# Layer 1 of a two-layer encoder: ten column pairs in two passes of block products instead of nine in three with an ordinary column, and the residual read in twelve portions

## The chip, the cores and the metric

The kernel runs on one core of a Trainium2 chip. The metric is device time in microseconds (us) of one execution, as the median of several runs of one compiled program. The engines: PE is TensorE (matmuls), DVE is VectorE, ACT is ScalarE, POOL is GpSimd, SP is SyncE, which here only issues DMAs. Each engine takes its instructions in the order of its own queue.

## The reference, cut to what matters

Two layers over 384 tokens (256 of a prompt, 128 of running streams) and a model width of 2048. Layer 0 is attention and is not touched. Layer 1, whose projections and gate the change is about, is

```
def c_project(h, w_in1, ln_g, ln_b):
    p = jnp.einsum('bsd,dn->bsn', h, w_in1)
    u = p[..., :C_WIDTH]
    v = layernorm(p[..., C_WIDTH:2 * C_WIDTH], ln_g, ln_b)
    z = p[..., 2 * C_WIDTH:]
    return u, v, z
...
u, v, z = c_project(rmsnorm(hp, norm1_g), w_in1, sgu_ln_g, sgu_ln_b)
mixed = spatial_mix(v...)
hp = hp + jnp.einsum('bsn,nd->bsd', u * mixed * jax.nn.silu(z), w_out1)
```

with C_WIDTH = 4096, all in fp32; `w_in1` is 2048 x 12288.

## The kernel before

**Precision.** A matmul takes operands of a shorter format (fp32r). Each fp32 operand is split into a high part (a copy by ScalarE, L90 or L84) and a low part (source minus high, by VectorE, L91 or L86), and each product is three matmuls: high by high, high by low, low by high. A token block is 128 of the 384 tokens (tb 0, 1, 2). A column is 512 of the 12288 columns of `w_in1`, so u, v and z have eight each, numbered 0 to 7.

**An ordinary column** (`dense_nat`, or `eight`, which cuts it into steps) takes 16 rows of blocks of 128 along the contraction, each with 3 token blocks and 3 matmuls: 144 matmuls of 128x128 by 128x512. Its weights come as `raw` tiles of 128x512.

**A pair of columns** is computed by `seven`, for columns a0 and a1 at once, by a Strassen scheme of the Winograd kind: token blocks 0 and 1 and the two halves of the contraction make 2 x 2 blocks, and seven block products (1 to 7) do for eight. Token block 2 is done beside them with four block products, p and q for column a0 and two into one bank, s, for a1. A block product is taken over four depths u, with 6 matmuls each (`stream`): 11 products x 4 x 6 = 264 matmuls for a pair, where two ordinary columns take 288. The weights come in wide tiles `sraw` of 128x1024 (512 KB, `load2`), some are added to each other by VectorE (L970), and each is split (`split2`) into `shi` and `slo`, four buffers of each. The sums of token blocks that the scheme needs are made once, before the stage, by `token_sums`, from the transposed and normalised activations `h1c`, and stay in `slot` and `suml` tiles; `row` and `tsum` give a product its tokens. For v pairs the statistics of the layer norm follow each result (L1041), for pairs of z and u the SiLU of z (ScalarE, L1055) and the product with u (VectorE, L898); results go to DRAM through POOL's queue (`vd`, `gd`).

**The stage.** Columns 0 and 1 of v are ordinary (from about 700 us to 780 us in the profile), and `token_sums` runs between the steps of the second. Then comes the pair stage, 780 to 1396 us: three v pairs (columns 2 to 7), then NP = 6 pairs of z and u (columns 0 to 5). A pair takes three passes: `singles` (products 1, p, 2, q), `chain` (5, s, 6, 4) and `pair` (3, s, 7), each over the four depths and each followed by a closing that brings its banks to the results. Column 6 of z and u is ordinary, and its 32 steps of 9 matmuls are strewn between the steps of the pairs by `some` and the numbers in `mix`; their `raw` tiles come through POOL's queue.

**What sets the order.** `run` prepares a step (loads, additions, splits) and issues the matmuls of the step before it. Below that a scheduler of the framework places the instructions in each engine's queue by its own estimate of when their operands are ready; `tc.issue_after` forbids it to place an instruction ahead of another one. Loads of `sraw` go through SP's queue and wait there for the release of one of the buffers (8 of 4 KB a partition).

**After the stage** come column 7 of z and u (ordinary), the spatial mixing in `prepare` (whose steps are hooked to the steps of other work by `hooked`), and the last projection `out1` in four pieces. The residual, saved in DRAM (`h1d`) in four column blocks, is read back by `residual_back`: one block at hook 15 of column 7, three more at hooks 3, 7 and 10 of the first `out1`, three DMAs each (L1285).

## Time and profile before

| | |
|---|---|
| median of 3 runs | 1756.37 us (1752.81 to 1758.05) |
| the profiled execution | 1750.52 us |
| its span, first to last instruction | 1748.8 us |
| granted TensorE clock, mean | 0.998 |
| busy: PE, DVE, ACT, POOL | 1733.6, 1258.0, 803.5, 383.7 us |
| weight loads of PE (PEld, beside the matmuls) | 1433.6 us |
| DMA | 416.02 MB, mean 238 GB/s |

Durations and places are read in the profiled execution, whose own time lies 5.9 us below the median; differences are made against it. The page gives the share of the span in which each engine is busy; windows of the trace give the same for a stretch. A group of instructions is given by line, engine, operation, output and inputs, with count, busy time, mean duration, and the idle time before it with what ended it. In the timeline a row has start, duration, engine, line, and instruction. PE's ends are modelled and its matmuls overlap, so its rate is read from the starts.

### The profile page before, as it was taken

What the parts mean: (1) busy time and instruction counts of PE and PEld (TensorE: products, weight loads), DVE (VectorE), ACT (ScalarE), POOL (GpSimd) and SP (SyncE); (2) the same over time, 40 slices, a digit from 0 to 9 for tenths busy, and PEclk for the clock granted to TensorE, in tenths of its full rate; (3) what the DMA queues carried; (4) which work ended last, traced back from release to release, by engine and by line L of the source; (5) the groups of instructions that cost most, each with busy time, mean ns of one, the idle gap of its engine ahead of it and who ended that gap; (6) DMA issues with size and microseconds to landing.
All of it is one profiled execution on the core that took longest, in us unless ns stands there. A gap on an engine that the chain in (4) does not pass through costs nothing. (4 is left out here: it accounts for less than half of the span.)

```text
span 1748.8 us, 24034 instructions
## 1 busy us (share of the span) xinstructions
PE 1733.6 (99%) x8347; PEld 1433.6 (82%) x8347; DVE 1258.0 (72%) x1773; ACT 803.5 (46%) x1237; POOL 383.7 (22%) x549
## 2 busy tenths in 40 slices
PE   9999999999999999999999999999999999999998
PEld 8988888888888888888888788888888888788887
DVE  6437566448348455588898998988999877777766
ACT  5435354337337344454444455444555433334344
POOL 6435544222212211110200010000000133423200
PEclk9999999999999999999999999999999999999999
DMA  8788989868877877678888987888888679778653
GB/s 232 189 225 198 280 215 215 246 178 207 240 205 194 257 187 163 188 266 297 257 269 274 308 293 258 273 282 260 288 292 288 210 238 332 234 222 309 179 158 114
DMA packets 229354, 416.02 MB, mean 238 GB/s; under 512 B 22552, under 2 KB 66128, under 8 KB 229232
## 3 DMA queue, kind: packets, MB, share of 16 engines
q1 hardware_dynamic: 166288, 295.62, 55.7%
q0 software_dynamic: 32112, 102.73, 21.2%
q10 hardware_dynamic: 30832, 16.13, 3.1%
q8 instruction: 65, 1.06, 0.3%
q14 instruction: 57, 0.47, 0.1%
HBM read 366.09 MB, written 48.29 MB: 237 GB/s over the span
## 5 line engine op out<-in xcount | busy, mean ns | idle before, releaser
L101 PE MATMUL d<-wlo,slot 128*128 128x512 f32 x1485 | 577.9, 390 | 0.0
L102 PE MATMUL d<-whi,slot 128*128 128x512 f32 x1485 | 577.3, 390 | 0.4 <-DVE slot L91 0.4
L86 DVE TENSOR_TENSOR wlo<-raw,whi 128x512 fp32r<-128x512 f32 x482 | 329.5, 695 | 315.3 <-ACT whi L84 311.4
L100 PE MATMUL d<-whi,slot 128*128 128x512 f32 x1485 | 531.4, 391 | 3.6 <-ACT whi L84 2.7
L84 ACT ACTIVATE whi<-raw 128x512 fp32r<-128x512 f32 x482 | 301.3, 629 | 495.8 <-PE d L102 396.1
L90 ACT ACTIVATE shi<-sraw 128x1024 fp32r<-128x1024 f32 x252 | 264.0, 1059 | 262.6 <-PE a L959 188.6
L100 PEld LDWEIGHTS d<-whi,slot 128*128 128x128 f32 x1485 | 279.1, 188 | 65.7 <-ACT whi L84 3.8
L102 PEld LDWEIGHTS d<-whi,slot 128*128 128x128 f32 x1485 | 279.1, 188 | 58.7 <-DVE slot L91 0.7
L101 PEld LDWEIGHTS d<-wlo,slot 128*128 128x128 f32 x1485 | 279.2, 188 | 58.4 <-DVE wlo L86 1.3
L91 DVE TENSOR_TENSOR slo<-sraw,shi 128x1024 fp32r<-128x1024 f32 x252 | 301.1, 1220 | 30.6 <-ACT shi L90 28.8
L958 PE MATMUL a<-slo,slot 128*128 128x512 f32 x720 | 280.8, 390 | 1.0 <-DVE slo L91 1.0
L957 PE MATMUL a<-shi,slot 128*128 128x512 f32 x720 | 265.8, 390 | 0.0
L959 PE MATMUL a<-shi,slot 128*128 128x512 f32 x612 | 237.7, 389 | 0.0
L970 DVE TENSOR_TENSOR sraw<-sraw,sraw 128x1024 f32<-128x1024 f32 x144 | 175.4, 1220 | 25.3 <-DMA sraw<-in_w_in_dram 24.9
L958 PEld LDWEIGHTS a<-slo,slot 128*128 128x128 f32 x720 | 135.1, 188 | 31.3 <-DVE slo L91 3.0
L957 PEld LDWEIGHTS a<-shi,slot 128*128 128x128 f32 x720 | 135.2, 188 | 28.9 <-DVE slot L970 0.5
L959 PEld LDWEIGHTS a<-shi,slot 128*128 128x128 f32 x612 | 114.9, 188 | 23.7
L464 POOL DMA_DIRECT2D slot<-d x48 | 44.1, 926 | 128.0 <-DVE wlo L86 54.2
L74 POOL DMA_DIRECT2D raw<-in_w_in_dram x32 | 17.6, 551 | 206.9 <-DVE wlo L86 202.7
L563 POOL DMA_DIRECT2D slot<-wd x32 | 27.2, 857 | 95.2 <-DMA wd<-pr 22.3
L970 DVE TENSOR_TENSOR slot<-a,slot 128x512 f32<-128x512 f32 x63 | 42.3, 684 | 1.9 <-PE a L959 1.7
L1057 POOL DMA_DIRECT2D gd<-slot x6 | 3.4, 566 | 182.7 <-DVE slot L898 122.3
(315 smaller groups left out, 1728.5 us busy)
## 6 DMA issues: line engine op xcount, KB each, us to landing
sraw<-in_w_in_dram SPq DMA_DIRECT2D x288, 512.0 KB, 5.0
raw<-in_w_in_dram SPq DMA_DIRECT2D x320, 256.0 KB, 3.9
raw<-in_w_out_dram SPq DMA_DIRECT2D x175, 256.0 KB, 4.2
slot<-d POOLq DMA_DIRECT2D x48, 192.0 KB, 5.8
raw<-in_w_in_dram POOLq DMA_DIRECT2D x32, 256.0 KB, 5.3
d<-slot ACTq DMA_DIRECT2D x24, 256.0 KB, 3.9
vd<-slot POOLq DMA_DIRECT2D x8, 768.0 KB, 6.7
gd<-slot POOLq DMA_DIRECT2D x8, 768.0 KB, 7.1
```

The lines of the kernel that those rows point to most:

```text
L84: highs.append(S.activation(hi, raw, AF.Copy).ins)
L86: splits.append(V.tensor_tensor(out=lo, in0=raw, in1=f32(hi), op=ALU.subtract).ins)
L90: S.activation(hi_out, src, AF.Copy)
L91: return V.tensor_tensor(out=lo_out, in0=src, in1=f32(hi_out), op=ALU.subtract).ins
L100: PE.matmul(o, lhsT=his[k][:, t], rhs=hi[:, 0, :], start=(k == first), stop=False)
L101: PE.matmul(o, lhsT=his[k][:, t], rhs=lo[:, 0, :], start=False, stop=False)
L102: mm = PE.matmul(o, lhsT=los[k][:, t], rhs=hi[:, 0, :], start=False, stop=(k == last))
L464: r = G.dma_start(blk[32 * j:32 * j + 32].rearrange("p h (a d) -> p (h a) d", d=32), d[:, :, 32 * j:32 * j + 32].rearrange("h (a p) d -> p ...
L957: PE.matmul(o, lhsT=xh, rhs=hi[:, j, :], start=(opens and u + j == 0), stop=False)
L958: PE.matmul(o, lhsT=xh, rhs=lo[:, j, :], start=False, stop=False)
L959: PE.matmul(o, lhsT=xl, rhs=hi[:, j, :], start=False, stop=(ends and u == 3 and j == 1))
L970: return V.tensor_tensor(out=out, in0=x, in1=y, op=op)
```

## The change

The column pairs become ten: NP = 7, so that column 6 of z and u is a pair as well, and no ordinary step is left in the stage (all numbers of `mix` are 0). The passes of a pair become two. The first has products 1, r, 2, r, 3 and 7, the second 5, s, 6, 4 and s, still 11 products and 264 matmuls. r is the whole of token block 2 for column a0 (p and q in one bank), and s is now the difference between column a1 and column a0 for that block, for which `token_sums` makes a fifth sum, t5, the difference of the two halves of token block 2. Each depth of the first pass makes one wide addition and four splits, each of the second three additions and three splits, where the three passes had 0, 3 and 1 additions and 2, 3 and 2 splits. The closings are four copies and one addition, and seven additions; before, they were two copies and two additions, three additions, and four. `issue_after` holds the second pass's additions and splits in turn.

`sraw` has seven buffers instead of eight, `suml` four instead of two; `shi` and `slo` lose the padding between 1024 and 2 x WPITCH = 1152 elements. `token_sums` takes four `sraw` buffers at a time instead of two. `residual_back` issues one DMA, and its twelve portions are hooked to steps 0 to 11 of the first `out1`.

The diff, without the bodies of the passes that go:

```diff
-            sums, spare = [], []
+            sums = []
             def wide():
-                return vp.tile([P, 2, 512], F32, tag="sraw", bufs=8, name=nm("sraw"))
+                return vp.tile([P, 2, 512], F32, tag="sraw", bufs=7, name=nm("sraw"))
             def token_sums(q):
                 hi, lo = h1c[q]
...
+                last, t5 = (x[:, 0] for x in (wide(), wide()))
+                t5 = t5[:, :2 * P].rearrange("p (j t) -> p j t", j=2)
+                last = last.rearrange("p (j h t) -> p j h t", h=2, t=P)
...
+                V.tensor_tensor(out=last.rearrange("p j h t -> p (j h) t"), in0=f32(hi[:, :, 2 * P:]), in1=f32(lo[:, :, 2 * P:]), op=ALU.add)
...
+                V.tensor_tensor(out=t5, in0=last[:, :, 0], in1=last[:, :, 1], op=ALU.subtract)
...
+                tl = vp.tile([P, 4, 2, P], F32R, tag="suml", bufs=4, name=nm("suml"))
+                t5h = x[:, 4]
+                t5l = x[:, 5]
+                for h, l, y in ((x[:, :4], tl, t), (t5h, t5l, t5)):
+                    S.activation(h, y, AF.Copy)
+                    V.tensor_tensor(out=l, in0=y, in1=f32(h), op=ALU.subtract)
+                sums.append(([x[:, i] for i in range(5)], [tl[:, i] for i in range(4)] + [t5l]))
             def row(tb, half):
...
             def split2(raw):
-                hi, lo = (vp.tile([P, 2 * WPITCH], F32R, tag=tag, bufs=4, name=nm(tag))[:, :1024].rearrange("p (j c) -> p j c", j=2) for tag in ("shi", "slo"))
+                hi, lo = (vp.tile([P, 1024], F32R, tag=tag, bufs=4, name=nm(tag)).rearrange("p (j c) -> p j c", j=2) for tag in ("shi", "slo"))
...
             def seven(a0, a1, row_done, stored):
...
-                m, second = {}, []
+                m = {}
                 def banks(*names):
...
                 def add(out, x, y, op=ALU.add):
...
-                def singles(u):
+                def first(u):
                     if u == 0:
-                        banks("1", "p", "2", "q")
-                    b11, b21 = split2(load2(u, 0, a0)), split2(load2(u, 1, a0))
+                        m["r"] = dbank()
+                        banks("1", "2", "3", "7")
+                    b11, b21, b22, b12 = load2(u, 0, a0), load2(u, 1, a0), load2(u, 1, a1), load2(u, 0, a1)
+                    w11 = split2(b11)
+                    with tc.issue_after(lows[-1]):
+                        add(b12, b22, b12)
+                    w21, w22, t3 = split2(b21), split2(b22), split2(b12)
                     def mul():
-                        stream(u, b11, (m["1"], row(0, 0), True, True), (m["p"], row(2, 0), True, True))
-                        stream(u, b21, (m["2"], row(0, 1), True, True), (m["q"], row(2, 1), True, True))
+                        stream(u, w11, (m["1"], row(0, 0), True, True), (m["r"], row(2, 0), True, False))
+                        stream(u, w21, (m["2"], row(0, 1), True, True), (m["r"], row(2, 1), False, True))
+                        stream(u, w22, (m["3"], tsum(3), True, True))
+                        stream(u, t3, (m["7"], tsum(2), True, True))
                     return mul
...
+                def close_first():
+                    for x, y in ((v1[:, 2], "1"), (v1[:, 0], "3"), (v1[:, 1], "7"), (v0[:, 2], "r")):
+                        S.activation(x, m[y], AF.Copy)
+                    add(v0[:, 0], m["2"], v1[:, 2])
+                    row_done(0, v0, v1, 0)
+
+                def second(u):
                     if u == 0:
                         banks("5", "s", "6", "4")
+                        done[:] = [lows[-1]] * 2
                     b11, b12, b22, b21 = load2(u, 0, a0), load2(u, 0, a1), load2(u, 1, a1), load2(u, 1, a0)
-                    add(b12, b12, b11, ALU.subtract)
-                    add(b22, b22, b12)
-                    add(b21, b22, b21, ALU.subtract)
-                    t1, t2, t4 = split2(b12), split2(b22), split2(b21)
+                    with tc.issue_after(done[0]):
+                        add(b12, b12, b11, ALU.subtract)
+                    with tc.issue_after(done[1]):
+                        add(b22, b22, b12)
+                    t1 = split2(b12)
+                    with tc.issue_after(lows[-1]):
+                        add(b21, b22, b21, ALU.subtract)
+                    t2 = split2(b22)
+                    done[0] = lows[-1]
+                    t4 = split2(b21)
+                    done[1] = lows[-1]
                     def mul():
-                        stream(u, t1, (m["5"], tsum(0), True, True), (m["s"], row(2, 0), True, False))
+                        stream(u, t1, (m["5"], tsum(0), True, True), (m["s"], tsum(4), True, False))
                         stream(u, t2, (m["6"], tsum(1), True, True))
-                        stream(u, t4, (m["4"], row(1, 1), True, True))
+                        stream(u, t4, (m["4"], row(1, 1), True, True), (m["s"], row(2, 1), False, True))
                     return mul
...
+                def close_second():
+                    add(v1[:, 2], m["6"], v1[:, 2])
+                    add(v0[:, 1], v1[:, 1], v1[:, 2])
+                    add(v1[:, 2], m["5"], v1[:, 2])
+                    add(v0[:, 1], v0[:, 1], m["4"], ALU.subtract)
+                    add(v1[:, 0], v1[:, 0], v1[:, 2])
+                    add(v1[:, 1], v1[:, 1], v1[:, 2])
+                    add(v1[:, 2], v0[:, 2], m["s"])
+                    for tb in (1, 2):
+                        row_done(0, v0, v1, tb)
                     for tb in range(NT):
                         row_done(1, v0, v1, tb)
                     stored(v0, v1)
-                return [(f, e) for f, e in ((singles, close_singles), (chain, close_chain), (pair, close_pair))]
+                done = []
+                return [(first, close_first), (second, close_second)]
             def v_pair(c):
...
-            NP = 6
+            NP = 7
...
             def some(n):
...
-                steps += [(part(0), u) for u in range(4)] + [(closing(0), None)]
-                for i, mix in ((1, (1, 1, 1, 0)), (2, (n % 3 != 1, 0, 0, 0))):
+                for i, mix in ((0, (0, 0, 0, 0)), (1, (0, 0, 0, 0))):
                     for u in range(4):
                         steps += some(mix[u]) + [(part(i), u)]
                     steps += [(closing(i), None)]
...
         def times(c, *whens):
...
-        def residual_back(c):
-            h1[c] = slot(F32).rearrange("p (t c) -> p t c", t=NT)
-            for tb in range(NT):
-                nc.sync.dma_start(h1[c][:, tb, :].rearrange("p (k d) -> p k d", k=4), h1d[c, :, tb * P:(tb + 1) * P, :].rearrange("k t d -> t k d"))
+        def residual_back(c, tb):
+            if tb == 0:
+                h1[c] = slot(F32).rearrange("p (t c) -> p t c", t=NT)
+            nc.sync.dma_start(h1[c][:, tb, :].rearrange("p (k d) -> p k d", k=4), h1d[c, :, tb * P:(tb + 1) * P, :].rearrange("k t d -> t k d"))
...
-        h[15] = lambda f=h[15]: [residual_back(0), f()] and None
...
         for tb in range(NT):
...
-            for i, c in ((3, 1), (7, 2), (10, 3)) if k0 == 0 else ():
-                h[i] = lambda f=h[i], c=c: [residual_back(c), f()] and None
+            for i in range(12) if k0 == 0 else ():
+                h[i] = lambda f=h[i], i=i: [residual_back(i // 3, i % 3), f()] and None
...
```

What moves in the queues, at three places. First TensorE, at the start of a pair (`a` and `d` are banks of PSUM, `shi` and `slo` split weights of a pair, `whi` and `wlo` those of the ordinary column, `slot` the tokens). Before:

```order
L957 MATMUL a_8740<-shi_8745,slot_6596 128x512
L958 MATMUL a_8740<-slo_8746,slot_6596 128x512
L959 MATMUL a_8740<-shi_8745,slot_6597 128x512
L101 MATMUL d_7813<-wlo_9684,slot_7282 128x512
L102 MATMUL d_7813<-whi_9682,slot_7283 128x512
L100 MATMUL d_7811<-whi_9988,slot_7282 128x512
L101 MATMUL d_7811<-wlo_9990,slot_7282 128x512
L102 MATMUL d_7811<-whi_9988,slot_7283 128x512
L100 MATMUL d_7812<-whi_9988,slot_7282 128x512
L957 MATMUL a_8739<-shi_8757,slot_6830 128x512
L957 MATMUL a_8740<-shi_8757,slot_6830 128x512
```

After:

```order
L959 MATMUL a_7937<-shi_8088,slot_7283 128x512
L957 MATMUL a_7937<-shi_8088,slot_7282 128x512
L958 MATMUL a_7937<-slo_8089,slot_7282 128x512
L959 MATMUL a_7937<-shi_8088,slot_7283 128x512
L958 MATMUL d_8168<-slo_8182,slot_6596 128x512
L959 MATMUL d_8168<-shi_8181,slot_6597 128x512
L957 MATMUL d_8168<-shi_8181,slot_6596 128x512
L958 MATMUL d_8168<-slo_8182,slot_6596 128x512
L959 MATMUL d_8168<-shi_8181,slot_6597 128x512
L957 MATMUL d_8168<-shi_8186,slot_6596 128x512
L958 MATMUL d_8168<-slo_8187,slot_6596 128x512
```

Before, steps of the ordinary column (L100 to L102, bank d) stand between the first products of the pair. Now a pair's last product (s, into a_7937) is followed at once by the next pair's first, which go into d_8168, its bank r.

Second VectorE, at about the same kind of place, the second pass of a pair (before: `chain`). L91 is a split, L970 with `sraw` a wide addition, L86 the split of an ordinary step. Before:

```order
L86 TENSOR_TENSOR wlo_9486<-raw_9482,whi_9484 128x512
L91 TENSOR_TENSOR slo_8453<-sraw_8439,shi_8452 128x1024
L970 TENSOR_TENSOR sraw_8531<-sraw_8531,sraw_8529 128x1024
L86 TENSOR_TENSOR wlo_9548<-raw_9544,whi_9546 128x512
L91 TENSOR_TENSOR slo_8507<-sraw_8497,shi_8506 128x1024
L970 TENSOR_TENSOR sraw_8533<-sraw_8531,sraw_8533 128x1024
L91 TENSOR_TENSOR slo_8511<-sraw_8499,shi_8510 128x1024
L91 TENSOR_TENSOR slo_8515<-sraw_8501,shi_8514 128x1024
L91 TENSOR_TENSOR slo_8539<-sraw_8529,shi_8538 128x1024
L86 TENSOR_TENSOR wlo_9684<-raw_9680,whi_9682 128x512
L91 TENSOR_TENSOR slo_8543<-sraw_8531,shi_8542 128x1024
L91 TENSOR_TENSOR slo_8547<-sraw_8533,shi_8546 128x1024
```

After, the last three depths of a second pass, the next pair's first splits, and the start of the closing (L970 with a slot and a bank):

```order
L91 TENSOR_TENSOR slo_8032<-sraw_8020,shi_8031 128x1024
L970 TENSOR_TENSOR sraw_8071<-sraw_8071,sraw_8069 128x1024
L91 TENSOR_TENSOR slo_8036<-sraw_8022,shi_8035 128x1024
L970 TENSOR_TENSOR sraw_8073<-sraw_8073,sraw_8071 128x1024
L91 TENSOR_TENSOR slo_8080<-sraw_8071,shi_8079 128x1024
L970 TENSOR_TENSOR sraw_8075<-sraw_8073,sraw_8075 128x1024
L91 TENSOR_TENSOR slo_8085<-sraw_8073,shi_8084 128x1024
L91 TENSOR_TENSOR slo_8089<-sraw_8075,shi_8088 128x1024
L91 TENSOR_TENSOR slo_8182<-sraw_8173,shi_8181 128x1024
L970 TENSOR_TENSOR sraw_8179<-sraw_8177,sraw_8179 128x1024
L91 TENSOR_TENSOR slo_8187<-sraw_8175,shi_8186 128x1024
L970 TENSOR_TENSOR slot_7680<-a_7938,slot_7680 128x512
```

Additions and splits now stand in turn, nothing else comes between them, and the closing's additions stand in turn with the next pair's splits.

Third SP, the DMA queue, at the residual (L1285 before, L1281 after; the `raw` loads are weights of the last projection). Before:

```order
L74 DMA raw_13391<-in_w_out_dram 128x512
L74 DMA raw_13435<-in_w_out_dram 128x512
L1285 DMA slot_13337<-h1d 128x4x128 x3
L1285 DMA slot_13505<-h1d 128x4x128
L74 DMA raw_13441<-in_w_out_dram 128x512
L1285 DMA slot_13505<-h1d 128x4x128 x2
L1285 DMA slot_13617<-h1d 128x4x128
L74 DMA raw_13475<-in_w_out_dram 128x512
L1285 DMA slot_13617<-h1d 128x4x128 x2
L74 DMA raw_13481<-in_w_out_dram 128x512
L74 DMA raw_13511<-in_w_out_dram 128x512
```

After:

```order
L74 DMA raw_13451<-in_w_out_dram 128x512
L74 DMA raw_13457<-in_w_out_dram 128x512
L1281 DMA slot_13353<-h1d 128x4x128 x3
L1281 DMA slot_13481<-h1d 128x4x128
L74 DMA raw_13493<-in_w_out_dram 128x512
L1281 DMA slot_13481<-h1d 128x4x128 x2
L1281 DMA slot_13593<-h1d 128x4x128 x3
L74 DMA raw_13499<-in_w_out_dram 128x512
L74 DMA raw_13526<-in_w_out_dram 128x512
```

The portions of the second to fourth column block stand behind the same number of weight loads as before, and nearly together.

More of the change, by code (lines that the diff above doesn't have):

```diff
@@ L918, in token_sums @@
                     V.tensor_tensor(out=t[:, i], in0=x, in1=y, op=ALU.subtract)
+                V.tensor_tensor(out=t5, in0=last[:, :, 0], in1=last[:, :, 1], op=ALU.subtract)
                 x = slot().rearrange("p (i j t) -> p i j t", j=2, t=P)
-                th = x[:, :4]
-                spare.append(x[:, 4:])
-                S.activation(th, t, AF.Copy)
-                if q in (1, 3):
-                    tl, n = spare[-2:], 2
-                else:
-                    tl, n = [vp.tile([P, 4, 2, P], F32R, tag="suml", bufs=2, name=nm("suml"))], 4
-                lows = []
-                for i, x in enumerate(tl):
-                    V.tensor_tensor(out=x, in0=t[:, i * n:i * n + n], in1=f32(th[:, i * n:i * n + n]), op=ALU.subtract)
-                    lows += [x[:, j] for j in range(n)]
-                sums.append(([th[:, i] for i in range(4)], lows))
+                tl = vp.tile([P, 4, 2, P], F32R, tag="suml", bufs=4, name=nm("suml"))
[5 more added lines that the diff above has]
+                sums.append(([x[:, i] for i in range(5)], [tl[:, i] for i in range(4)] + [t5l]))
             def row(tb, half):
@@ L977, in mul @@
                     def mul():
-                        stream(u, b11, (m["1"], row(0, 0), True, True), (m["p"], row(2, 0), True, True))
-                        stream(u, b21, (m["2"], row(0, 1), True, True), (m["q"], row(2, 1), True, True))
-                    return mul
-                def close_singles():
-                    S.activation(v1[:, 0], m["1"], AF.Copy)
-                    S.activation(v1[:, 2], m["p"], AF.Copy)
-                    add(v0[:, 0], m["2"], v1[:, 0])
-                    add(v0[:, 2], m["q"], v1[:, 2])
-                    for tb in (0, 2):
-                        row_done(0, v0, v1, tb)
@@ L1010, in pair @@
-                def pair(u):
-                    if u == 0:
-                        m["3"] = dbank()
-                        banks("7")
-                    b22, b12 = load2(u, 1, a1), load2(u, 0, a1)
-                    with tc.issue_after(second[-1]):
-                        add(b12, b22, b12)
-                    w = split2(b22)
-                    second.append(lows[-1])
-                    t3 = split2(b12)
-                    def mul():
-                        stream(u, w, (m["3"], tsum(3), True, True), (m["s"], row(2, 1), False, True))
-                        stream(u, t3, (m["7"], tsum(2), True, True))
-                    return mul
@@ L1026, in close_pair @@
-                def close_pair():
-                    add(v1[:, 0], m["3"], v1[:, 1])
-                    add(v1[:, 2], m["s"], v1[:, 2])
-                    add(v0[:, 1], m["7"], v0[:, 1])
-                    add(v1[:, 1], m["7"], v1[:, 1])
-                    row_done(0, v0, v1, 1)
+                def close_second():
[8 more added lines that the diff above has]
+                        row_done(0, v0, v1, tb)
```

5 lines of the change are left out of this document (removed).

## The prediction

> **What bounds the kernel now.** I read the page's table of engines first, then the stretch that the change rewrites, in windows.
>
> ```profile
> PE 1733.6 (99%) x8347; PEld 1433.6 (82%) x8347; DVE 1258.0 (72%) x1773; ACT 803.5 (46%) x1237; POOL 383.7 (22%) x549
> ```
>
> ```profile
> core 0: us, PE busy (x) PEld busy (x) DVE busy (x) ACT busy (x) POOL busy (x), PEclk, DMA share, GB/s
> 740.00:780.00 40.00, 40.00 (x178) 33.14 (x177) 33.34 (x52) 21.22 (x31) 4.12 (x8) 1.00 0.71 238
> 780.00:1396.00 616.00, 614.20 (x2697) 504.87 (x2696) 551.78 (x557) 305.69 (x326) 45.21 (x74) 1.00 0.84 276
> 950.00:1000.00 50.00, 49.42 (x215) 39.68 (x214) 48.75 (x52) 25.32 (x26) 1.65 (x3) 1.00 0.86 287
> 1200.00:1250.00 50.00, 49.62 (x220) 40.72 (x219) 46.18 (x47) 25.09 (x28) 1.11 (x2) 1.00 0.83 271
> ```
>
> TensorE is busy 99% of the span, so only fewer matmuls, or fewer of its small gaps, can shorten the run. The stretch from 780 to 1396 us is the pair stage. TensorE idles 616.00 - 614.20 = 1.8 us there, and VectorE (DVE) is already busy for 551.78 of 616 us, 90%. The third and fourth windows show what happens when VectorE comes close to full: at 48.75 of 50 us TensorE loses 0.58 us, at 46.18 of 50 it loses 0.38. So the stage is TensorE's by a thin margin, and that margin is the question of this case.
>
> How long one matmul holds TensorE is not its duration (0.39 us, pipelined) but the distance of starts, which the timeline gives:
>
> ```profile
> 784.86 0.39 PE L957 MATMUL a<-shi,slot 128*128 128x512 f32 x1
> 785.08 0.39 PE L958 MATMUL a<-slo,slot 128*128 128x512 f32 x1
> ...
> 793.92 0.39 PE L958 MATMUL a<-slo,slot 128*128 128x512 f32 x1
> ```
>
> Between the first and the last of these rows lie 40 starts without a gap: 9.06 / 40 = 0.2265 us each.
>
> **TensorE's work.** Before, nine pairs of 264 matmuls (11 products, 4 depths, 6 each) and 288 ordinary ones: 2376 + 288 = 2664. After, ten pairs: 2640. It is 24 matmuls less, 24 x 0.2265 = **5.4 us** off the path that sets the end. That is the whole direct gain. The tenth pair saves little because one pair of 264 takes the place of 288.
>
> **VectorE's work.** These groups are the whole of it in the stage:
>
> ```profile
> L91 DVE TENSOR_TENSOR slo<-sraw,shi 128x1024 fp32r<-128x1024 f32 x250 | 298.7, 1220 | 30.4 <-ACT shi L90 28.5 <-DMA sraw<-in_w_in_dram 1.0
> L970 DVE TENSOR_TENSOR sraw<-sraw,sraw 128x1024 f32<-128x1024 f32 x144 | 175.4, 1220 | 25.3 <-DMA sraw<-in_w_in_dram 24.9
> L970 DVE TENSOR_TENSOR slot<-a,slot 128x512 f32<-128x512 f32 x61 | 41.1, 684 | 1.9 <-PE a L959 1.7
> L86 DVE TENSOR_TENSOR wlo<-raw,whi 128x512 fp32r<-128x512 f32 x36 | 24.3, 684 | 2.4 <-ACT whi L84 2.4
> L898 DVE SCALAR_TENSOR_TENSOR slot<-slot,rstd,slot 128x512 f32<-128x512 f32 x17 | 12.6, 746 | 0.1
> L1041 DVE BATCH_NORM_STATS2 stats<-slot 128x6 f32<-128x512 f32 x18 | 12.0, 685 | 0.0
> ```
>
> The last three are the closings and evictions. A pair has 28 splits (L91) and 16 wide additions (L970), 44 instructions of 1.220 us, before and after alike: each depth has 7 splits and 4 additions in either form. The closings have 9 additions of 0.684 before and 8 after. A v pair adds 6 statistics of 0.685, a z and u pair 3 gatings of 0.746. Before, the ordinary steps add 32 x 0.684 = 21.9 us. By durations before: 9 x (53.7 + 6.2) + 3 x 4.1 + 6 x 2.2 + 21.9 = 586.5 us. After: 10 x (53.7 + 5.5) + 3 x 4.1 + 7 x 2.2 = 619.7 us, 33 more, against 2640 x 0.2265 = **598 us** of matmuls. Added up so, VectorE would need 22 us more than TensorE.
>
> But the window has 551.78 busy us where the sum of durations gives 586.5. Instructions that follow each other overlap in their records:
>
> ```profile
> 968.71 1.22 DVE L970 TENSOR_TENSOR sraw<-sraw,sraw 128x1024 f32<-128x1024 f32 x1
> 969.85 5.76 DVE L91 TENSOR_TENSOR slo<-sraw,shi 128x1024 fp32r<-128x1024 f32 x5
> 975.52 1.22 DVE L970 TENSOR_TENSOR sraw<-sraw,sraw 128x1024 f32<-128x1024 f32 x1
> ```
>
> From 968.71 to 969.85, and five times up to 975.52, the starts lie 1.135 us apart, not 1.220. So I scale by what was measured: 551.8 / 586.5 = 0.941, and 619.7 x 0.941 = **583 us**, 97.5% of TensorE's 598. VectorE does not become the bound on average, but what was 90% becomes 97.5%, which is the load of the window 950 to 1000.
>
> [...]
>
> **What the load costs TensorE.** No row shows ten pairs in a row at 97.5%, so I bound it from the windows. Lower end: none, even the 1.8 us of before go, since in the order of the changed kernel each split still stands ahead of its matmuls, and 24.9 us of VectorE's waits for wide loads can go. Upper end: the 0.58 us per 50 us of the window 950 to 1000 throughout, 598 / 50 x 0.58 = 6.9 us. One depth of the second pass is the tight place: 6 VectorE instructions x 1.135 = 6.8 us against 30 matmuls x 0.2265 = 6.8 us. The first pass gives 36 x 0.2265 = 8.15 us for 5 x 1.135 = 5.7, and four split buffers carry that lead over. I take 3 us, between the two ends, 1.2 more than before.
>
> The new waits are at the two closings of a pair. The seven additions that close the second pass wait for its last products, and behind them on VectorE stand the splits of the next pair, in turn with them. TensorE meanwhile has the products of the two splits ahead of them, 24 matmuls or 5.4 us, half of them into the bank for r, which nothing has to free; the first closing addition (bank 6) frees the bank that the other half needs first. By these sums each new product's bank comes free about 2 us before it is wanted. From the first pass to the second it is closer, 0.5 to 0.8 us, with ScalarE's copy (four closing copies now stand in its queue) ahead of VectorE's split. I cost both at 0, inside the 3 us.
>
> The waits on loads:
>
> ```profile
> DVE slo L91 <- ACT shi L90: 28.5, 35, 1.7
> DVE sraw L970 <- DMA sraw<-in_w_in_dram: 24.9, 29, 2.7
> ```
>
> ```profile
> sraw<-in_w_in_dram SPq DMA_DIRECT2D x288, 512.0 KB, 5.0
> ```
>
> Seven wide buffers instead of eight look worse, but the additions now stand between the splits. From the release of a buffer (its split) to the first use of the next load in it, the order leaves mostly six or more VectorE instructions, 6 x 1.135 = 6.8 us, against 5.0 us to landing; before it was often three or four, 3.4 to 4.5 us, hence the 29 waits. Demand grows from 276 GB/s to about 276 x 616 / 598 x 1.05 = 299 (320 loads of 512 KB for 288, the 32 of 256 KB gone: 5% more bytes). I cost this at nothing; if the landing rises to 7.5 us, each wait is about 0.7 us of VectorE that its 15 us of reserve no longer hide (third rival).
>
> **The start of the stage.** token_sums gets, for each of four blocks, an addition of 128x512, a subtraction and a split of 128x256, one copy on ScalarE, and two more wide buffers, and two of its splits are joined:
>
> ```profile
> L918 DVE TENSOR_TENSOR sraw<-sraw,sraw 128x256 f32<-128x256 f32 x8 | 3.4, 419 | 0.1
> L929 DVE TENSOR_TENSOR slot<-sraw,slot 128x512 fp32r<-128x512 f32 x4 | 2.6, 690 | 1.4 <-ACT slot L922 1.4
> ```
>
> ```profile
> 770.00:780.00 10.00, 10.00 (x46) 8.29 (x45) 9.35 (x14) 7.13 (x10) 2.50 (x6) 1.00 1.04 395
> ```
>
> That is 4 x (0.69 + 0.42 + 0.42) = 6.1 us, less 2 x 0.15 for the joined splits, 5.8 us in a stretch where VectorE has 40 - 33.34 = 6.7 us free, and where the order also puts four splits of the last dense column, 4 x 0.69 = 2.8 us. 8.6 - 6.7 = 1.9 us too much. Between 770 and 780 VectorE has 0.65 us free and the DMA engines none (share 1.04), and the first loads of the stage now wait for buffers that token_sums holds. Ends: 0 (the lead of the ordinary column hides it) and 4 us (all that does not fit, twice). I take **2 us**, the overflow itself.
>
> **The residual.** The twelve portions are hooked one by one, but in SyncE's queue they stand 3, then 11 weight loads, then 4, 1 and 5 nearly together, as before. What bounds that place:
>
> ```profile
> 1439.43 1.52 SPq L1285 DMA_DIRECT2D slot<-h1d  x3
> 1465.60 5.31 SPq L1285 DMA_DIRECT2D slot<-h1d  x4
> ```
>
> ```profile
> 1490.00:1500.00 10.00, 7.25 (x32) 5.71 (x32) 7.88 (x14) 2.69 (x5) 5.30 (x9) 1.00 1.02 282
> 1500.00:1510.00 10.00, 10.00 (x40) 8.08 (x40) 6.44 (x12) 4.32 (x8) 0.58 (x1) 0.83 0.80 274
> ```
>
> TensorE loses 2.7 us at 1495 and then runs ten us at a granted clock of 0.83, 1.7 us more: 4.4 us. The same bytes go through the same queue at the same places, so I cost the edit at 0, with ends of -4.4 (the stall goes) and +4.4 (it comes twice). Buffers without padding, and the 32 raw loads that leave POOL's queue (POOL is 22% busy) show in no row as a cost to TensorE; 0 for both, and nothing in the trace tells a sign.
>
> **The sum.** -5.4 + 1.2 + 2 + 0 = **-2.2 us**. The profiled run took 1750.5 us, which gives 1748.3; it lies 5.9 below the median of 1756.4, so on the median's scale **1754.2**.
>
> **Rivals.** First, better: the stage loses no more than before, nothing at its start, and the tail's stall goes: -5.4 - 4.4 = -9.8, 1746.5. For it: the removed load waits; against it: the queue's order. Second, slower: VectorE becomes the bound, at the second pass of each pair, as soon as its instructions cannot overlap (an addition must see the result of the addition before it, a split its ScalarE copy). Price: 619.7 us instead of 603 + 1.8, +14.6, with the start +16.6: 1773; half of it, where only the second passes lose it, 1764.7. It decides as soon as starts there lie over 1.16 us apart (598 / 583 x 1.135). For it: the 28.5 us of waits on ScalarE's copies; against it: the row of starts. Third: loads come late with seven buffers at 299 GB/s, one uncovered wait of 0.7 us per pair, 10 x 0.7 = 7, 1754.2 + 7 = 1761. Fourth, the residual edit does not spread its loads: this is in the forecast already.
>
> **Chances.** Forecast (1749 to 1759) 0.50; first rival 0.17; second 0.18; third 0.15. 0.3% of 1756.4 is 5.3 us, about what a measurement of this kernel can tell from no change, so faster means below 1751.1 and slower above 1761.7. Faster: 0.17 and 0.17 of the forecast's 0.50, 0.34. Slower: 0.18 and 0.06 of the third, 0.24; the rest, 0.42, is no change. The range goes from the first rival's 1746 to 1768, inside the second.
>
> **What would show it.** TensorE's matmuls in the pair stage 24 fewer; VectorE's share there 0.97 or more; the waits of L970 for loads well under 24.9 us; TensorE's idle time in the stage 3 us and near the stage's start 2 us; the 2.7 us stall in the tail still there. I am wrong if VectorE's starts in the second pass lie 1.2 us apart, if TensorE waits for slo at every pass boundary, or if the tail's stall moves by several us.

## The result and the profile after

| | before | after |
|---|---|---|
| first comparison, median | 1755.98 us (1752.81 to 1758.05, 4 runs) | 1742.74 us (1741.97 to 1744.27, 4 runs) |
| repeated in a later job, median | 1750.98 us (1746.38 to 1757.10, 27 runs) | 1741.75 us (1740.92 to 1745.11, 10 runs) |
| profiled execution | 1750.52 us | 1743.44 us |

The ratio is 0.9933 (95% interval 0.9912 to 0.9955) in the first comparison and 0.9956 (0.9943 to 0.9970) in the second: the change makes the kernel faster by 0.3 to 0.9%. Forecast was 1754.2, in a range of 1746 to 1768, with no change as the likeliest; the time lies below the range.

The two traces differ by 7.1 us. To see where, I take TensorE's time at four places of its order. In the next rows, of the instructions of one line, the two times at the end are the first and the last start: the first and last product of the pairs (L957), the first spatial product (L1242 before, L1238 after), and the first product with `wlast` (L1358, L1353). Before:

```profile
L957 PE MATMUL a<-shi,slot x720: 387/389/499, 780.6 to 1395.1; 128*128 128x512 f32 x180
L1242 PE MATMUL a<-vh,wTh x32: 277/334/396, 1418.0 to 1653.9; 128*128 128x512 f32 x16, 128*128 128x256 f32 x16
L1358 PE MATMUL d<-wlast,slot x33: 389/389/396, 1707.3 to 1736.2; 128*128 128x512 f32 x33
```

After:

```profile
L957 PE MATMUL a<-shi,slot x720: 387/389/504, 782.3 to 1398.5; 128*128 128x512 f32 x180
L1238 PE MATMUL a<-vh,wTh x32: 277/388/502, 1419.6 to 1646.5; 128*128 128x512 f32 x16, 128*128 128x256 f32 x16
L1353 PE MATMUL d<-wlast,slot x33: 389/389/396, 1700.2 to 1729.1; 128*128 128x512 f32 x33
```

With the number of TensorE's instructions between these places in the order of each program, and 0.2265 us for one, the difference splits so (us):

| stretch | before | after | difference | of it instructions | rest |
|---|---|---|---|---|---|
| to the first pair product | 780.6 | 782.3 | +1.7 | 0 | +1.7 |
| first to last pair product | 614.5 (2689) | 616.2 (2695) | +1.7 | +1.4 | +0.3 |
| to the first spatial product | 22.9 (101) | 21.1 (93) | -1.8 | -1.8 | 0 |
| to the first `wlast` product | 289.3 (1266) | 280.6 (1244) | -8.7 | -5.0 | **-3.7** |
| to the end of the execution | 43.2 | 43.2 | 0 | 0 | 0 |
| all | 1750.5 | 1743.4 | -7.1 | **-5.4** | -1.7 |

The counts sum to the 24 matmuls that go. That they go from the last stretches, though the change is in the pairs, is the scheduler's doing: it now places 30 matmuls of column 7 inside the pair stage. The 1.7 us ahead of the stage are scatter: in seven traces of the kernel before and of its variants with the same passes (they follow below) the first pair product starts at 780.6 to 785.3 us and the stage takes 613.7 to 616.5, in four traces of the changed kernel and its variants 780.9 to 782.4 and 615.7 to 616.2. So the pair stage itself runs at the pace of before, and the rest of the gain is behind it, at the stall that the prediction had left in place.

The page and windows of after, with the columns as before:

```profile
PE 1728.0 (99%) x8323; PEld 1426.8 (82%) x8323; DVE 1290.0 (74%) x1794; ACT 828.2 (48%) x1259; POOL 363.6 (21%) x517
```

```profile
780.00:1390.00 610.00, 608.01 (x2669) 498.89 (x2668) 579.24 (x566) 332.98 (x350) 22.60 (x35) 1.00 0.88 295
950.00:1000.00 50.00, 50.00 (x221) 41.07 (x220) 48.92 (x51) 27.24 (x27) 6.43 (x7) 1.00 0.94 316
1200.00:1250.00 50.00, 50.00 (x222) 41.21 (x221) 47.46 (x48) 28.43 (x31) 0.53 (x1) 1.00 0.86 290
1490.00:1500.00 10.00, 10.00 (x46) 8.29 (x45) 9.38 (x17) 4.59 (x9) 4.10 (x8) 1.00 1.04 285
1500.00:1510.00 10.00, 10.00 (x48) 8.31 (x48) 5.81 (x11) 2.56 (x5) 1.32 (x3) 1.00 0.76 271
```

VectorE is busy for 579.24 of 610 us, 95%, up from 90%, and TensorE idles 1.99 us there, about as much as before: in the window 950 to 1000 VectorE has 48.92 of 50 us and TensorE all 50. The last two rows are the place of the stall of before: no idle time, and the clock at 1.00.

VectorE's two largest groups in the stage, and its waits for loads:

```profile
L91 DVE TENSOR_TENSOR slo<-sraw,shi 128x1024 fp32r<-128x1024 f32 x279 | 335.3, 1219 | 25.3 <-ACT shi L90 24.1
L970 DVE TENSOR_TENSOR sraw<-sraw,sraw 128x1024 f32<-128x1024 f32 x160 | 195.1, 1219 | 4.6 <-DMA sraw<-in_w_in_dram 4.3
```

The counts are those of the prediction (280 and 160 for ten pairs). The waits for loads have gone from 24.9 us to 4.3. The timeline of a second pass, with additions and splits in turn:

```profile
944.15 1.22 DVE L91 TENSOR_TENSOR slo<-sraw,shi 128x1024 fp32r<-128x1024 f32 x1
945.29 1.22 DVE L970 TENSOR_TENSOR sraw<-sraw,sraw 128x1024 f32<-128x1024 f32 x1
...
957.78 1.22 DVE L91 TENSOR_TENSOR slo<-sraw,shi 128x1024 fp32r<-128x1024 f32 x1
```

From 944.15 to 957.78 lie 12 starts, 13.63 / 12 = 1.136 us each, although most of them need the result of an addition: the records, of 1.22 us each, overlap in the tight pass too. It doesn't try a closer dependence: in this order no instruction needs the result of the one right before it.

### The profile page after: what moved, and what is told of

It reads as the page before. It is cut to its first block, busy times and chain, and to the rows that moved or that the text cites. A ratio compares the mean times of both kernels' runs of the same rounds, so it can differ in the third digit from the quotient of the medians.

```text
span 1741.7 us, 23995 instructions
## 1 busy us (share of the span) xinstructions
PE 1728.0 (99%) x8323; PEld 1426.8 (82%) x8323; DVE 1290.0 (74%) x1794; ACT 828.2 (48%) x1259; POOL 363.6 (21%) x517
## 5 line engine op out<-in xcount | busy, mean ns | idle before, releaser
L101 PE MATMUL d<-wlo,slot 128*128 128x512 f32 x1389 | 540.5, 390 | 0.2
L102 PE MATMUL d<-whi,slot 128*128 128x512 f32 x1389 | 539.8, 390 | 0.3 <-DVE slot L91 0.3
L86 DVE TENSOR_TENSOR wlo<-raw,whi 128x512 fp32r<-128x512 f32 x450 | 310.4, 700 | 306.4 <-ACT whi L84 305.1
L84 ACT ACTIVATE whi<-raw 128x512 fp32r<-128x512 f32 x450 | 281.5, 630 | 457.2 <-PE d L102 363.4
L100 PE MATMUL d<-whi,slot 128*128 128x512 f32 x1389 | 493.9, 391 | 0.8 <-ACT whi L84 0.6
L90 ACT ACTIVATE shi<-sraw 128x1024 fp32r<-128x1024 f32 x280 | 296.0, 1061 | 265.5 <-DVE sraw L970 115.5
L91 DVE TENSOR_TENSOR slo<-sraw,shi 128x1024 fp32r<-128x1024 f32 x280 | 336.6, 1220 | 25.5 <-ACT shi L90 24.1
L100 PEld LDWEIGHTS d<-whi,slot 128*128 128x128 f32 x1389 | 260.4, 188 | 59.2 <-issue 1.8
L102 PEld LDWEIGHTS d<-whi,slot 128*128 128x128 f32 x1389 | 260.7, 188 | 54.9 <-DVE slot L91 0.7
L957 PE MATMUL a<-shi,slot 128*128 128x512 f32 x720 | 264.8, 391 | 1.4 <-ACT shi L90 1.2
L970 DVE TENSOR_TENSOR sraw<-sraw,sraw 128x1024 f32<-128x1024 f32 x160 | 195.1, 1219 | 4.6 <-DMA sraw<-in_w_in_dram 4.3
L957 PEld LDWEIGHTS a<-shi,slot 128*128 128x128 f32 x720 | 135.0, 188 | 34.2 <-ACT shi L90 5.0
L959 PE MATMUL a<-shi,slot 128*128 128x512 f32 x400 | 155.7, 389 | 0.0
L959 PE MATMUL a<-shi,suml 128*128 128x512 f32 x320 | 124.5, 389 | 0.0
L959 PEld LDWEIGHTS a<-shi,slot 128*128 128x128 f32 x400 | 75.1, 188 | 15.8
L959 PEld LDWEIGHTS a<-shi,suml 128*128 128x128 f32 x320 | 60.1, 188 | 12.5
L957 PE MATMUL d<-shi,slot 128*128 128x512 f32 x160 | 62.3, 389 | 0.0
```

Of the source, the lines that this page charges most:

```text
L84: highs.append(S.activation(hi, raw, AF.Copy).ins)
L86: splits.append(V.tensor_tensor(out=lo, in0=raw, in1=f32(hi), op=ALU.subtract).ins)
L90: S.activation(hi_out, src, AF.Copy)
L91: return V.tensor_tensor(out=lo_out, in0=src, in1=f32(hi_out), op=ALU.subtract).ins
L100: PE.matmul(o, lhsT=his[k][:, t], rhs=hi[:, 0, :], start=(k == first), stop=False)
L101: PE.matmul(o, lhsT=his[k][:, t], rhs=lo[:, 0, :], start=False, stop=False)
```

## The experiments

Each job also ran the kernel before, whose median was 1750.5 to 1751.5 us in all of them. So the 1756 of the first comparison is high for it, and times below are read against 1751. The changed kernel itself was measured twice, at 1742.74 and 1741.75 us; differences to it below are to 1741.75 and mostly across jobs, so about 1 us of them can be scatter.

**The kernel before again**, without an edit, twice.

> The kernel before, unchanged, for a second trace. Of the 13.2 us by which the medians differ the two profiled executions show 7.1 only, and the profiled one of before is the shortest of its runs. Theory A (TensorE loses more in most executions of before than in the one that was profiled, in the tail): about 1756 us, TensorE's gaps after 1396 us and what it loses to a clock under 1.0 there together over 8 us, the pair stage as in the first trace, idle under 2.5 us. Theory B (the executions of before differ in the pair stage): the same time, but idle of 4 us or more between 780 and 1396 us. Theory C (the spread is outside the span): a span near 1749 us again with a longer time around it.

> The kernel before, a third trace. Theory A: the stretch after the first spatial product 289 to 292 us, as in its two traces so far (289.3, 290.3), with a clock under 1.0 after the stall. Theory B (the stall comes and goes): about 285 us.

They took 1754.7 and 1756.15 us. The stretch from the first spatial product to the first `wlast` product was 290.3 and 293.0 us, after 289.3 in the first trace, and the pair stage 615.3 and 614.7, after 614.5. The third trace, at the stall:

```profile
L1242 PE MATMUL a<-vh,wTh x32: 277/334/396, 1419.9 to 1658.5; 128*128 128x512 f32 x16, 128*128 128x256 f32 x16
L1358 PE MATMUL d<-wlast,slot x33: 389/389/396, 1712.9 to 1741.8; 128*128 128x512 f32 x33
```

```profile
1500.00:1510.00 10.00, 6.71 (x20) 5.01 (x20) 5.33 (x11) 3.18 (x6) 0.85 (x2) 0.66 0.86 318
```

TensorE waits 3.29 us in these ten, and the clock granted is 0.66. The stall is not chance of one execution: three of three have it, of 2.0 to 3.6 us of waiting for `whi`, and a low clock (0.83, 0.83 and 0.66 from 1500 to 1510). It doesn't explain all of the spread. Of the 5.6 us between the first and the third trace 3.7 lie in that stretch; of the 4.2 us between the first and the second only 1.0 does, 2.4 lie before the pair stage and 0.8 in it, so none of the three theories for the second trace holds as it stands.

**The residual alone, and undone.**

```diff
 before, with residual_back(c, tb) of the change:
-        h[15] = lambda f=h[15]: [residual_back(0), f()] and None
-            for i, c in ((3, 1), (7, 2), (10, 3)) if k0 == 0 else ():
+            for i in range(12) if k0 == 0 else ():
 and the reverse in the changed kernel
```

> The kernel before with the change of the residual alone (twelve portions hooked to steps 0 to 11 of the first last-projection piece, none at step 15 of column 7). Theory A (the residual's reads cause the tail's stall and low clock): 4 to 8 us faster than before, ratio 0.995 to 0.998, and no stall of 2.7 us after 1440 us. Theory B (the queue holds the portions in the same places, so nothing moves): ratio 0.999 to 1.001 and the stall still there.

> The changed kernel with the residual read as before (four blocks, the first at step 15 of column 7). Theory A: it loses what the residual gives, 4 to 8 us, so ratio 0.996 to 0.998 to the kernel before. Theory B: as the changed kernel, ratio 0.992 to 0.994.

Alone: 1752.93 us, ratio 1.0002 (0.9989 to 1.0015). Undone: 1743.19 us, ratio 0.9955 (0.9942 to 0.9967). The residual edit is worth nothing, in either kernel, and it doesn't remove the stall: alone, the stretch took 291.2 us with the stall; undone, 281.1 without it.

**Ten pairs alone, two passes alone.** Before, with NP = 7:

```diff
-            NP = 6
+            NP = 7
```

> The kernel before with ten pairs instead of nine and no ordinary steps (NP = 7), all else as it was: three passes, eight wide buffers, padded split buffers, the residual in four blocks. It has the 24 matmuls less. Theory A (the gain is these matmuls, and the rest is the tail): 5.4 us faster, ratio 0.996 to 0.998. Theory B (the two passes are needed for it, since three passes without ordinary steps between starve TensorE on VectorE): not faster, ratio 1.000 or more, with TensorE idle 5 us or more in the pair stage. Theory C (all of the gain is from the tenth pair): ratio 0.992 to 0.994.

1754.06 us, ratio 1.0014 (1.0004 to 1.0024): slower than before, with 24 matmuls less.

```profile
L957 PE MATMUL a<-shi,slot x800: 387/389/504, 781.3 to 1401.2; 128*128 128x512 f32 x160
```

```profile
800.00:900.00 100.00, 94.69 (x403) 74.56 (x402) 95.04 (x96) 47.08 (x47) 11.21 (x19) 1.00 0.88 286
```

```profile
DVE sraw L970 <- DMA sraw<-in_w_in_dram: 22.2, 23, 3.8
```

The stage takes 619.9 us for 2665 instructions, 16.3 us over 2665 x 0.2265; in the changed kernel 616.2 is 5.8 over its 610.4, before 614.5 is 5.4 over 609.1. VectorE's load is that of the changed kernel (580.50 us from 780 to 1390), but its waits for loads are still 22.2 us, and its work is uneven: in `chain` a depth has 6 x 1.135 = 6.8 us of VectorE against 24 x 0.2265 = 5.4 of TensorE, which the ordinary steps had filled up. Which of the two makes the loss, no run separates. More than half of it is the start of the stage: the window 800 to 900 has 403 matmuls, where 100 / 0.2265 = 441 fit, so 8.7 of the 16.3 us are lost there; the changed kernel has 427 in the same window, 3.3 us short.

The changed kernel with nine pairs:

```diff
-            NP = 7
+            NP = 6
-                for i, mix in ((0, (0, 0, 0, 0)), (1, (0, 0, 0, 0))):
+                for i, mix in ((0, (1, 1, 0, 0)), (1, (1, n % 3 != 1, 0, 0))):
```

> The changed kernel with nine pairs: column 6 of z and u is ordinary again (NP = 6) and its steps stand at the first two depths of each pass; two passes as in the change. Theory A (ten pairs save the 24 matmuls, and two passes only make that possible): 5 us over the changed kernel, about 1748, ratio 0.997 to 1.000. Theory B (two passes are a gain of their own, since VectorE's work is spread evenly): as the changed kernel or at most 3 us over it, ratio 0.995 to 0.997. TensorE idle in the pair stage under 2 us in both.

1749.39 us, ratio 0.9994 (0.9982 to 1.0007). So neither half does it alone (about +3.5 and -1.6 us), and both together do (-9.2). Two passes are worth 12.3 us with ten pairs (1754.06 to 1741.75), and 11 of that is the pair stage (16.3 to 5.3 us over its instructions, in the second trace of the changed kernel). The tenth pair is worth 7.6 us with two passes, 5.4 of it the matmuls. Two passes stand here for all that the change does to the passes, the forced turn and the seven buffers included. With nine pairs the stall is there:

```profile
1490.00:1500.00 10.00, 7.80 (x35) 6.13 (x33) 7.94 (x14) 2.22 (x4) 5.52 (x10) 1.00 1.02 271
1500.00:1510.00 10.00, 9.64 (x37) 7.88 (x38) 5.92 (x11) 4.92 (x9) 0.58 (x1) 0.83 0.80 278
```

From the first spatial product to the first `wlast` product both kernels have 1244 instructions; nine pairs take 286.5 us for them, ten 280.6.

The traces of the four kernels say where each half counts. The table has the pair stage and the stretch after it, each less 0.2265 us for every instruction in it (a few matmuls of the second, of 128x256, are shorter: in the trace of before three of them start at 1419.40, 1419.51 and 1419.63 us; hence values under 0):

| | pair stage | over its instructions | first spatial to first `wlast` product | over its instructions |
|---|---|---|---|---|
| nine pairs, three passes (before) | 614.5 (2689) | 5.4 | 289.3 (1266) | 2.6 |
| ten pairs, three passes | 619.9 (2665) | 16.3 | 285.8 (1266) | -0.9 |
| nine pairs, two passes | 618.5 (2719) | 2.6 | 286.5 (1244) | 4.7 |
| ten pairs, two passes (after) | 616.2 (2695) | 5.8 | 280.6 (1244) | -1.2 |

The lines of the two middle rows, first ten pairs in three passes (its stage stands above), then nine in two:

```profile
L1242 PE MATMUL a<-vh,wTh x32: 277/335/499, 1424.1 to 1655.7; 128*128 128x512 f32 x16, 128*128 128x256 f32 x16
L1358 PE MATMUL d<-wlast,slot x33: 389/389/396, 1709.9 to 1738.8; 128*128 128x512 f32 x33
```

```profile
L957 PE MATMUL a<-shi,slot x648: 389/389/501, 782.4 to 1400.9; 128*128 128x512 f32 x162
L1238 PE MATMUL a<-vh,wTh x32: 277/388/505, 1422.0 to 1654.8; 128*128 128x512 f32 x16, 128*128 128x256 f32 x16
L1353 PE MATMUL d<-wlast,slot x33: 389/389/396, 1708.5 to 1737.4; 128*128 128x512 f32 x33
```

With the 5.4 us of the 24 matmuls these add up to +2.0, -0.7 and -8.8 us against before, beside the medians' +3.5, -1.6 and -9.2. So the tenth pair costs some time in the stage, 11 us in three passes and 3 in two, and takes away the stall in either form; two passes are what makes its cost small.

**The changed kernel again.**

> The changed kernel, unchanged, beside the kernel before on this chip, on which the medians of before have been 1750.5 us instead of 1756. Theory A (the first comparison's 13 us hold 6 us in which the kernel before ran longer for reasons of its own, DMA above all, and the change gives the 7 us that the two traces show): 1743 us, ratio 0.995 to 0.997. Theory B (the change gives 13 us): ratio 0.992 to 0.994.

1741.75 us. The gain is 7 to 9 us against the 1751 of the kernel before in these jobs, nearer to the traces' 7.1 than to the first 13. Its runs lie within 4.2 us of each other, those of before beside it within 10.7.

**What holds up the weight loads in the tail.** The residual's reads moved from SP's queue to POOL's, in three kernels:

```diff
-            nc.sync.dma_start(h1[c][:, tb, :]...
+            G.dma_start(h1[c][:, tb, :]...
```

> The kernel before with the twelve reads of the residual in POOL's queue instead of SP's, so that no weight load waits behind them for a free slot. Theory A (the tail's stall and low clock come from SP's queue being held up by these reads, from 1465.6 to 1478.4 us in the first trace): 3 to 5 us faster, ratio 0.997 to 0.998, weight loads going on through that stretch and no wait of TensorE for whi there. Theory B (the DMA engines are full there, so the bytes cost what they cost): ratio 0.999 to 1.001.

> The kernel before with the residual through POOL's queue, a second trace, since its first trace was its shortest execution (1748.1 us) and its median 1752.4. Theory A: stretch after the first spatial product about 285.3 us again (22 rows longer than in two passes, 5 us), no low clock, and what it loses lies before 1400 us. Theory B (the short stretch was chance): 289 to 292 us, as the kernel before.

> The changed kernel with the reads of the residual in POOL's queue. Theory A (in the changed kernel the queue resumes early enough, and nothing of the stall is left): as the changed kernel, within 1 us. Theory B (1.6 us of TensorE's idle time at 1450 to 1500 us is still that stall): 1 to 2 us faster than the changed kernel. If POOL's own chain for the spatial mixing is delayed by the reads, slower by some us.

> Nine pairs in two passes (as in nine_pairs_two_passes, 1749.4 us, whose stretch from the first spatial product to the first wlast product took 286.5 us where ten pairs take 280.5 for the same rows), with the residual read through POOL's queue. Theory A (the 4 to 6 us that nine pairs lose there come from weight loads held behind the reads in SP's queue): stretch 280 to 281.5 us, no clock under 1.0 there, median 1744 to 1746. Theory B (the reads are not it): stretch about 286 us, median 1748 to 1750. If the stretch is short in the trace and the median is not, other executions lose their time elsewhere.

In the kernel before, the stretch is then 285.3 us in one trace and 285.7 in the other, after 289.3, 290.3 and 293.0 with SP's queue. The second:

```profile
L1242 PE MATMUL a<-vh,wTh x32: 277/335/501, 1420.2 to 1651.9; 128*128 128x512 f32 x16, 128*128 128x256 f32 x16
L1358 PE MATMUL d<-wlast,slot x33: 389/389/396, 1705.9 to 1734.8; 128*128 128x512 f32 x33
```

The two profiled executions took 1748.3 and 1749.9 us. But the median of the 12 runs was 1752.43, ratio 1.0008 (0.9995 to 1.0021): what the traces show gone is not gone from the median. With nine pairs in two passes the stretch fell from 286.5 to 283.1 us and the median from 1749.39 to 1747.55 (ratio 0.9980, 0.9970 to 0.9989, an interval that overlaps the one without the move; theory A had 280 to 281.5 us and 1744 to 1746). In the changed kernel nothing moved: 1742.12. So the reads in SP's queue take part in the stall, and moving them is worth 0 to 2 us of time, not 4.

**The padding of the split buffers**, removed in the kernel before:

```diff
-                hi, lo = (vp.tile([P, 2 * WPITCH], ...)[:, :1024]
+                hi, lo = (vp.tile([P, 1024], ...)
```

> The kernel before with its split buffers shi and slo without padding (1024 elements instead of 1152), nothing else. Theory A (padding costs and gives nothing): ratio 0.999 to 1.001. Theory B (part of the changed kernel's 8 us is the new addresses): 2 us or more faster, ratio under 0.999.

1751.73 us, ratio 1.0004 (0.9990 to 1.0018): nothing.

**The turn of additions and splits**, taken away in the changed kernel:

```diff
-                    with tc.issue_after(done[0]):
-                        add(b12, b12, b11, ALU.subtract)
-                    with tc.issue_after(done[1]):
-                        add(b22, b22, b12)
+                    add(b12, b12, b11, ALU.subtract)
+                    add(b22, b22, b12)
                     t1 = split2(b12)
-                    with tc.issue_after(lows[-1]):
-                        add(b21, b22, b21, ALU.subtract)
+                    add(b21, b22, b21, ALU.subtract)
```

> The changed kernel without the three issue_after of the second pass, which hold its additions and splits in turn; the scheduler places the additions. Theory A (the turn is what makes the second pass fit, since six VectorE instructions stand against 30 matmuls with nothing to spare): 3 to 15 us slower than the changed kernel, TensorE idle over 4 us in the pair stage. Theory B (two passes of 36 and 30 matmuls a depth fit in any order): within 1.5 us of the changed kernel, 1742 to 1744.

1748.51 us, 6.8 over the changed kernel, ratio 0.9985 (0.9975 to 0.9995).

```profile
800.00:900.00 100.00, 95.44 (x409) 75.61 (x409) 91.42 (x91) 49.96 (x52) 11.16 (x19) 1.00 0.90 287
1100.00:1200.00 100.00, 100.00 (x443) 82.81 (x442) 95.84 (x91) 56.34 (x60) 1.07 (x2) 1.00 0.89 301
```

TensorE loses 4.56 us from 800 to 900, with VectorE busy for 91.42 of 100 us, and nothing from 1100 to 1400, although VectorE has 95.84 of 100 from 1100 to 1200. VectorE's waits for loads are 10.7 us instead of 4.3. So the turn matters in the first pairs.

**Six wide buffers** in the changed kernel (`bufs=7` to `bufs=6` for `sraw`):

> The changed kernel with six wide load buffers instead of seven. Theory A (the changed order leaves slack for loads, so the waits for loads fell from 24.9 us to 4.3 us on VectorE, and one buffer less takes about 1.1 us of that slack from each): VectorE's waits for loads 10 to 30 us, TensorE idle up to 5 us more, 1743 to 1748. Theory B (load slack is not what limits): within 1 us of the changed kernel.

1748.00 us, 6.2 over the changed kernel, and the runs spread over 6.5 us.

```profile
DVE sraw L970 <- DMA sraw<-in_w_in_dram: 16.8, 18, 3.5
```

VectorE's waits for loads are back at 16.8 us. Six buffers are too few for this order; whether an eighth would help was not tried. Before, eight left 24.9 us of such waits.

**token_sums earlier** in the changed kernel:

```diff
-... for q, kp in enumerate((2, 6, 10, 14))}))
+... for q, kp in enumerate((0, 2, 6, 10))}))
```

> The changed kernel with token_sums hooked to steps 0, 2, 6 and 10 of column 1 instead of 2, 6, 10 and 14, so that VectorE has that work behind it four steps of 18 matmuls (8 us) earlier. Theory A (the start of the stage costs 1.5 to 2 us, because VectorE is full from 740 to 850 us): 1 to 2 us faster than the changed kernel, TensorE idle between 780 and 860 us under 0.5 us. Theory B (the start's loss is the lead that VectorE has to build up in the first pair at 95% load, whenever token_sums runs): within 0.7 us.

1740.78 us (1739.95 to 1741.38), ratio 0.9941 (0.9926 to 0.9955), the lowest median, though its interval overlaps that of the changed kernel (0.9943 to 0.9970). TensorE's idle time from 800 to 900 us, first in the changed kernel, then here:

```profile
800.00:900.00 100.00, 98.11 (x427) 79.04 (x426) 94.19 (x93) 50.71 (x53) 11.16 (x19) 1.00 0.92 297
```

```profile
800.00:900.00 100.00, 99.15 (x436) 80.97 (x435) 95.02 (x94) 52.45 (x54) 11.19 (x19) 1.00 0.92 295
```

1.9 us of idle time become 0.85; from 780 to 830 there is none. The median is 1.0 us lower, between the two theories and no more than two jobs can differ. So part of the start's cost is VectorE's full stretch, as the forecast had it; that the rest is the lead is likely, not shown.

## Why the prediction was wrong

On the scale of the traces the forecast was 1748.3 us and the trace took 1743.4, 4.9 less: 3.7 from the tail, 2.9 from the stage and its start, less the 1.7 of scatter ahead of the stage. On the scale of the medians 6.6 us more came from the step between the two.

- **24 matmuls, 5.4 us.** Right: it is the instruction column of the table.
- **VectorE at 97.5% and not the bound.** Right in kind: it is busy for 580 us in the stage, where the forecast had 583, with starts 1.136 us apart. (The six rows that it calls the whole of this work are 564 of the 582.6 us of its window by durations; its sum of 586.5 counts the rest as well.) Its share is only 94 to 95%, since 55 matmuls that belong to no pair stand in the stage too. The price, 3 us of idle time between bounds of 0 and 6.9 and 2 more at the start, was too high: these terms put the stage 3.2 us above before, and beyond its instructions it took 0.3 more (5.8 us instead of 5.4), start included. The upper bound came from windows of before in which load waits and uneven passes fell together with the load; in the window 950 to 1000 the load alone, 48.92 of 50 us, costs TensorE nothing. That it costs so little hangs on two details, the turn (6.8 us) and the seventh buffer (6.2 us), which the forecast did not price by themselves.
- **Loads at nothing.** Right: 24.9 us of waits became 4.3, with one buffer less.
- **The start, 2 us.** Right in size for the idle time, 1.9 us in the first trace, at 800 to 900 instead of 780; but what the rest of the stage saved against before pays for it.
- **The residual at 0, its portions still bunched.** Right for the edit, by the two runs on it.
- **The tail, "the same bytes go through the same queue at the same places, so I cost the edit at 0".** This step failed. The edit was worth 0, but the stall behind it was taken as given, while it hangs on the reads in SP's queue and on the order of all the rest, which the scheduler made anew for ten pairs. All six traces with nine pairs and the reads in SP's queue have it, none of the seven with ten pairs has, and none of the three of nine pairs with the reads in POOL's queue. It is 3.7 us of the first traces' 7.1, and it came by luck: the edit that was meant for this place did nothing. The first rival had both the stall's end and a stage that loses no more, at 0.17; its -9.8 us, from 1751, gives 1741.2, against 1741.75 measured. How ten pairs escape the stall stays open. The weight loads after the reads resume 57.8 to 58.5 us after the first spatial product with ten pairs in two passes and 59.5 with nine; in three passes 61.6 with ten and 62.4 to 63.7 with nine. In each form the kernel with the later time has the stall, but no one time parts the four, and no run moved the weight loads alone.
- **From the trace to the median, +5.9 us.** This step failed too, and for the number it is the larger one. The 5.9 us by which the three runs of before lay above its profiled one were carried over to the changed kernel, whose median lay 0.7 below its own. They were those of one job: in the four later jobs the median of before is 0.0 to 0.9 us above that profiled execution. From 1751 the forecast's -2.2 us would have given 1748.8, still 7 us too slow. The runs of before do spread over 5 to 12 us in every job, those of the changed kernel over 2 to 4; since moving the reads shortened the tail but neither the median nor the spread (8.4 us), what makes up the rest isn't settled.

## What to carry to other kernels

When work is taken from an engine that fills the gaps of another, compare the load of the feeding engine pass by pass, not over the stage: at the same 95% three uneven passes cost 16 us over their matmuls, more than half of it at the start, and two even ones with their forced turn 6, though no run parts the evenness from the order. A load buffer or a forced order is worth pricing alone when the feeding engine has little reserve (here, with VectorE at 95%, 6.2 and 6.8 us). And before a forecast is moved from a profiled execution to a median, ask whether the spread belongs to something that the change touches.

## What the runs showed of the hardware

At this stall TensorE loses time twice, in the wait and at a low clock. In the first trace of before TensorE waits 2.7 us for `whi`, until 1499.76, and from 1501 us on the granted clock is 0.50. The third trace, whose wait of 3.3 us ended at 1503.77, has the low clock already during the wait. The first trace, then two windows of the third (TensorE busy, clock, DMA share, GB/s):

```profile
1502.00:1504.00 2.00, 2.00 (x6) 0.50 1.04 335
1502.00:1504.00 2.00, 0.23 (x1) 0.50 1.01 413
1504.00:1508.00 4.00, 4.00 (x10) 0.50 1.02 349
```

In windows of 1 us the time at 0.50 adds up to 3.4 us in the first trace and to 6.8 in the third, 2.1 of them before the wait is over. By the starts that follow the waits, 15 take 5.14 us and 12 take 5.04, so against 0.2265 us for one the low clock costs 1.7 and 2.3 us. The second trace, whose longest wait for `whi` is only 1.8 us, has a mean clock of 0.83 from 1500 to 1510, as the first. In the changed kernel 1.6 us of idle time from 1460 to 1470, with no wait over 1.1 us, go by at a clock of 1.00. What sets the length of the low clock, no run shows.

VectorE keeps starts 1.136 us apart for records of 1.22 through the pass shown above, with additions and splits in turn, where each result is used two or more instructions later.
